# The mLSTM core of a hybrid layer: operands split into fp16 halves instead of fp32r halves, with one measured scale per head, and the query products ahead of the states

## The chip, the cores and the metric

The kernel runs on one core of one Trainium2 chip. The metric is the device time of one execution in microseconds (us); lower is better. Before the change three runs gave 1850.2, 1853.77 and 1854.75 us, the median is 1853.77. One further execution was profiled.

Engines: TensorE (PE; its weight loads are shown as PEld), VectorE (DVE), ScalarE (ACT), GpSimd (POOL) and SyncE (SP). SP issues most DMAs; a DMA that ScalarE issues stands in ScalarE's own instruction order (ACTq in the profile).

## The reference

One layer over 1024 latent tokens and 256 context tokens of width 1024, everything in fp32: a modulated norm, one input projection that feeds two branches (windowed attention and a bidirectional mLSTM), a gated merge, and a convolutional feed-forward block. What the change touches is the mLSTM, which runs in chunks of 128 tokens, in both directions, for 4 heads with 128 columns of query and key and 256 of value:

```python
def step(carry, xs):                       # one chunk of 128 tokens, one direction
    Cm, n, m = carry                       # state C (128 x 256), n (128), m
    ...
    s = jnp.einsum('bthd,bshd->bhts', qc, kc) * jnp.exp(dmat - m_t[..., None])
    num = (jnp.einsum('bhts,bshv->bthv', s, vc)
           + jnp.einsum('bthd,bhdv->bthv', qc, Cm) * w_inter.transpose(0, 2, 1)[..., None])
    nq = s.sum(axis=-1) + w_inter * jnp.einsum('bthd,bhd->bht', qc, n)
    den = jnp.maximum(jnp.abs(nq), jnp.exp(-m_t))
    h = num / den.transpose(0, 2, 1)[..., None]
    ...
    C_new = decay[..., None, None] * Cm + jnp.einsum('bshd,bshv->bhdv', kc * wk, vc)
    n_new = decay[..., None] * n + jnp.einsum('bshd->bhd', kc * wk)
```

The context chunks run first and give each direction its starting state; afterwards `h` of both directions is added, normalised per head (root mean square) and multiplied by a sigmoid gate.

## The kernel before, in words

The program has a start-up, an attention stage, the mLSTM stage (`stage_mlstm`, about 605 to 965 us of the trace) and a tail (`stage_tail`: the branch products yb and the feed-forward block).

Precision comes from halves: each operand x is split into hi = round(x) on ScalarE (`copy_act`, seen in the profile as L47) and lo = x - hi on VectorE (L54, or L56 where a scale is applied on the way). `mm3` (L158 to L165) then issues three matmuls for each product: hi.hi, hi.lo, lo.hi. Projection weights and the layer's input hT have fp16 halves that are scaled by a measured number. In the mLSTM core the halves of q, k, v, of the decayed scores and of the states are fp32r (32-bit) tiles.

Per head h, the stage does this, with the tile names that the profile shows:

- `prepare`, `load_kv`: load the weights (wrw_ml, wrw_mlqo), square them on ScalarE for their scale (wjw), split them (whkv, wlkv; whqo, wlqo).
- `proj_kv`: eight latent blocks, each 24 matmuls of 384 columns into a PSUM bank kv, of which there are two in turn. ScalarE takes out k and VH, VectorE VL. The two context blocks come by DMA as k and vr.
- `trans_k`: transposes of k into kT, split into kh, kl.
- `states`: the first two steps of each direction: kwh (GpSimd) and kwl (VectorE) are k times a decay, in halves; dC is their product with V; C is updated by VectorE and split into CH, CL.
- `proj_q`: q products in two banks of 512 columns, split into qh, ql.
- `core`: S = q.k in two banks; ub = S times decays (VectorE, L1460), split into sh, sl; then for each of eight blocks and both directions o (scores times V), i (q times state), nm (their sum and the division), hf (result), and the next dC, C, CH, CL.
- `proj_o`: the gate products mo, 96 matmuls of 512 columns, which the program writes behind the core and the scheduler places partly between the core's own products.
- `readout`, `turn`: squares of hf (rj), transposes mt, gate multiplication mo, stores to mlT_d on SP.
- `masked`, `decays`: the decay matrices ub of the next head, by DMA, an addition and 16 exponentials on ScalarE.
- `branch_sums`: sums of weights and activations for the tail (s_ba, t_at, s_bm); their loads are issued by ScalarE, into two buffers in turn, and their stores by SP.

The stage is written head by head in this order, and a scheduler that simulates the program orders every engine's instructions from it: each engine then executes its list strictly in order. The list depends on modelled durations, on priorities by program order and on when SBUF space is free, since pools of the next stage lie where earlier tiles lay. The tail's operand loads (baar, bawr on SP, L1717; sga on ScalarE's queue, L1748) wait for such space.

Of the kernel before, what the change touches and what calls it, by code (L numbers as in the profile page):

```python
# [348 lines left out]
def stage_startup(E, at):  # L349
# [3 lines left out]
    with ExitStack() as st:  # L353
# [198 lines left out]
        for i in range(4):  # L552
# [50 lines left out]
            for c in range(NCB):  # L603
                ps = pcx[c]
                kvx = wp.tile([P, 388], F32, tag="kvx", name=f"kvx{i}_{c}", bufs=3)
                a, z = i * 388, (i + 1) * 388
                mk, mv = min(max(512 - a, 0), 388), min(1536 - a, 388)
                if mk > 0:
                    copy_act(nc, kvx[:, :mk], ps[:, :mk], scale=DQK ** -0.5)
                    nc.sync.dma_start(E.kx_d[c][:, a : a + mk], kvx[:, :mk])  # L610
                if mk < mv:
                    nc.vector.tensor_copy(kvx[:, mk:mv], ps[:, mk:mv])
                    nc.sync.dma_start(E.vx_d[c][:, a + mk - 512 : a + mv - 512], kvx[:, mk:mv])
                if mv < 388:
                    nc.vector.tensor_tensor(E.gtile[:, c], ps[:, mv:388], E.gb, op=ALU.add)


def stage_attention(E, st, at):
# [343 lines left out]
    def gate_math():  # L962
# [102 lines left out]
        E.GC = dict(u_d=u_d, dec=dec, col=lambda nm, r: call[:, cols[nm] + r : cols[nm] + r + 1])  # L1065
# [36 lines left out]
    def early_act(j, ps):  # L1102
        E.kv0[j] = E.kvp.tile([P, 384], F32, name=f"kv0_{j}")
        copy_act(nc, E.kv0[j], ps[:, :384], scale=RAW["wf", NKV][:, 4:5])
# [146 lines left out]
def stage_mlstm(E, st):  # L1251
    nc, tc, A, ident, expo, hT, w2, dr = E.nc, E.tc, E.A, E.ident, E.expo, E.hT, E.w2, E.dr
    mm_tile, tp_tile, s_tile, mlT_d, gtile = E.mm_tile, E.tp_tile, E.s_tile, E.mlT_d, E.gtile

    E.turn_banks(3)
# [4 lines left out]
    vp = st.enter_context(tc.tile_pool(name="mlv", bufs=13, reuse_waits="tile"))  # L1260

# [6 lines left out]
    nc.gpsimd.memset(ones2[:, 0:1], 1.0)  # L1268

    def b512(name):  # L1270
        return bp.tile([P, 512], F32R, tag="b512", name=name)
# [8 lines left out]
    def v_tiles(h, j, src, scale=None):  # L1280
        vh = vp.tile([P, DVA], F32R, tag="VH", name=f"VH{h}_{j}")
        vl = vp.tile([P, DVA], F32R, tag="VL", name=f"VL{h}_{j}")
        nc.gpsimd.tensor_copy(vh[:, DV:DVA], ones2[:, 0:2])
        nc.gpsimd.tensor_copy(vl[:, DV:DVA], ones2[:, 2:4])
        split_from(nc, vh[:, 0:DV], vl[:, 0:DV], src, scale=scale)
        return vh, vl

    def prepare(h):
        H.setdefault(h, {})
        if h == 0:  # L1290
            H[h].update(w_ml=E.wml0, w_mlqo=E.wqo0)
# [16 lines left out]
    def proj_kv(h):  # L1308
        w, f = H[h].pop("wkv"), H[h]["fkv"]
        ks, vs = [None] * NBLK, [None] * NBLK  # L1310
        for j in orders(h)[0][1]:
            k = kp.tile([P, DQK], F32, tag="k", name=f"k{h}_{j}")
            if j < NCB:
                nc.sync.dma_start(k, E.kx_d[j][:, h * DQK : (h + 1) * DQK])
                vr = kp.tile([P, DV], F32, tag="vr", name=f"vr{h}_{j}", bufs=2)
                nc.sync.dma_start(vr, E.vx_d[j][:, h * DV : (h + 1) * DV])
                vs[j] = v_tiles(h, j, vr)
            elif h == 0 and j - NCB in E.kv0:
                kv = E.kv0[j - NCB]
                copy_act(nc, k, kv[:, 0:DQK], scale=DQK ** -0.5)  # L1320
                vs[j] = v_tiles(h, j, kv[:, 128:384])
            else:
                ps = mm_tile(f"kv{h}_{j}")
                mm3(nc, ps[:, :384], hT, w, sl((j - NCB) * P, P), sl(0, 384))
                kc = copy_act(nc, k, ps[:, 0:DQK], scale=f[:, 5:6])
                vs[j] = v_tiles(h, j, ps[:, 128:384], f[:, 4:5])
# [8 lines left out]
    def proj_q(h):  # L1335
# [4 lines left out]
        for t in range(2):  # L1340
# [3 lines left out]
            split_from(nc, qh, ql, ps, scale=f[:, 4:5])  # L1344
# [66 lines left out]
    def states(h):  # L1411
# [3 lines left out]
        CHL = [{}, {}]  # L1415

        def update(d, i, c):
# [3 lines left out]
            kh = wp.tile([P, DQK], F32R, tag="kwh", name=f"kwh{nm}", bufs=3)  # L1421
            kl = wp.tile([P, DQK], F32R, tag="kwl", name=f"kwl{nm}", bufs=3)
            wk = col("wK", r)
            E.kw = nc.gpsimd.tensor_scalar(kh, ks[c], wk, 1.0, op0=ALU.mult, op1=ALU.mult)  # L1424
            nc.vector.scalar_tensor_tensor(kl, ks[c], wk, kh.bitcast(F32), op0=ALU.mult, op1=ALU.subtract)
# [20 lines left out]
    def core(h):  # L1446
# [11 lines left out]
        for t, d in [(i ^ d, d) for i in range(2) for d, _ in orders(h)]:  # L1458
            Dm = DM.pop((h, t, d))
            nc.vector.tensor_tensor(Dm, pS[t].rearrange("p (c t) -> p c t", c=4)[:, :: (1, -1)[d]], Dm, op=ALU.mult)  # L1460
# [4 lines left out]
        def output(d, i, c, first):  # L1465
# [8 lines left out]
            num = wp.tile([P, 260], F32, tag="num", name=f"nm{nm}", bufs=3)  # L1474
            nc.scalar.activation(num[:, :257], pi[:, :257], AF.Copy, scale=col("wI", r))
            nc.vector.tensor_tensor(num[:, :257], num[:, :257], ps[:, :257], op=ALU.add)
            nq = num[:, 256:257]
            nc.vector.scalar_tensor_tensor(num[:, 257:258], nq, -1.0, col("em", r), op0=ALU.mult, op1=ALU.max)
# [20 lines left out]
    def readout(h):  # L1499
        hf, sgs = H[h]["hf"], H[h]["sg"]  # L1500
        for t in halves(h):
# [6 lines left out]
            nc.gpsimd.tensor_scalar(rr[:, 0:4], rr[:, 0:4], 1.0 / DV, EPS, op0=ALU.mult, op1=ALU.add)  # L1508
# [61 lines left out]
    for h in range(MLH):  # L1570
# [866 lines left out]
```

## Time and profile before

| | |
|---|---|
| runs | 1853.77 us median (1850.2 to 1854.75) |
| profiled execution | 1858.65 us, of which the span of the trace is 1856.9 |
| busy share of the span | PE 97%, DVE 76%, ACT 58%, POOL 27% |
| TensorE's granted clock, mean | 0.987 |
| mLSTM stage | about 605 to 965 us |
| heads' cores, first S to last o or i | about 631 to 671, 733 to 765, 825 to 863 and 920 to 953 us |

Two things matter in reading it. TensorE's matmuls overlap, so a busy TensorE is not one at its peak: the interval from one start to the next is the price of a matmul, not its duration. And the granted clock falls to one half for some us after TensorE has stood still, so a stall costs more than its own length. In a row of the groups stand the busy time and the mean duration in ns, then the idle time of that engine ahead of it, and what ended it.

### The profile page before, as it was taken

What the parts mean: (1) busy time and instruction counts of PE and PEld (TensorE: products, weight loads), DVE (VectorE), ACT (ScalarE), POOL (GpSimd) and SP (SyncE); (2) the same over time, 40 slices, a digit from 0 to 9 for tenths busy, and PEclk for the clock granted to TensorE, in tenths of its full rate; (3) what the DMA queues carried; (4) which work ended last, traced back from release to release, by engine and by line L of the source; (5) the groups of instructions that cost most, each with busy time, mean ns of one, the idle gap of its engine ahead of it and who ended that gap; (6) DMA issues with size and microseconds to landing.
All of it is one profiled execution on the core that took longest, in us unless ns stands there. A gap on an engine that the chain in (4) does not pass through costs nothing.

```text
span 1856.9 us, 27874 instructions
## 1 busy us (share of the span) xinstructions
PE 1795.2 (97%) x9207; PEld 1286.0 (69%) x9207; DVE 1418.6 (76%) x2864; ACT 1070.7 (58%) x2229; POOL 510.5 (27%) x747
## 2 busy tenths in 40 slices
PE   7889999999998899989999999999999999999999
PEld 3855555555555565656668887878888888888887
DVE  3848878888788685858687787698988998896665
ACT  4747777878787564646356563375444444464441
POOL 2467769687762630303020021000000000000000
PEclk9899999999999899999999999999999999999999
DMA  8647988888787724260449936413454544599751
GB/s 336 234 138 147 195 174 177 190 179 196 148 181 138 217 94 161 79 210 32 148 160 359 362 101 221 168 57 125 159 211 180 186 172 154 197 321 369 262 171 68
DMA packets 302193, 342.47 MB, mean 184 GB/s; under 512 B 176208, under 2 KB 200672, under 8 KB 299232
## 3 DMA queue, kind: packets, MB, share of 16 engines
q1 hardware_dynamic: 287648, 314.47, 56.1%
q10 hardware_dynamic: 14400, 26.22, 4.3%
q8 instruction: 72, 1.18, 0.3%
q14 instruction: 73, 0.60, 0.1%
HBM read 224.61 MB, written 76.16 MB: 162 GB/s over the span
## 4 chain that ended last, share of the span: by engine, by line
PE 77%; DVE 7%; DMA 5%; ACT 5%; issue 4%; POOL 3%; ACTq 0%; SPq 0%; POOLq 0%; DVEq 0%
PE g L706 8%; PE pq L706 6%; PE pa L2015 4%; PE pa L2017 4%; PE pa L2016 4%; PE po L706 3%; PE dx L2015 2%; PE dx L2017 2%; PE dx L2016 2%; PE pb L2017 2%; PE pb L2016 2%; PE pb L2015 2%; PE yb L2015 2%; PE yb L2016 2%; PE yb L2017 2%
## 5 line engine op out<-in xcount | busy, mean ns | idle before, releaser
L850 DVE CUSTOM_DVE_ANT_0 s<-s,maskA,nsink 128x640 f32<-128x640 f32 (+1 forms) x128 | 117.5, 918 | 75.0 <-PE s L845 74.6
L866 DVE TENSOR_TENSOR P<-s,P 128x640 f16<-128x640 f32 (+1 forms) x128 | 100.7, 787 | 1.0 <-ACT s L861 1.0
L860 ACT ACTIVATE P<-s,st 128x640 f16<-128x640 f32 (+1 forms) x128 | 98.3, 768 | 4.2
L706 PE MATMUL g<-hH,fh 128*128 128x512 f16 x256 | 97.9, 382 | 0.0
L706 PE MATMUL g<-hH,fl 128*128 128x512 f16 x256 | 97.8, 382 | 0.0
L706 PE MATMUL g<-hL,fh 128*128 128x512 f16 x256 | 97.7, 382 | 0.0
L861 ACT ACTIVATE s<-s,st 128x640 f32<-128x640 f32 (+1 forms) x128 | 93.9, 734 | 0.0
L706 PEld LDWEIGHTS <-hH 128*128 128x128 f16 x640 | 62.1, 98 | 36.5 <-DVE t L770 0.4
L858 ACT ACTIVATE st<-st,shift 128x1 f32<-128x1 f32 x128 | 37.6, 294 | 85.4 <-DVE st L850 84.7
L706 PE MATMUL pq<-wha,hH 128*128 128x384 f16 (+1 forms) x256 | 83.9, 328 | 0.1
L706 PE MATMUL pq<-wha,hL 128*128 128x384 f16 (+1 forms) x256 | 83.9, 328 | 0.0
L706 PE MATMUL pq<-wla,hH 128*128 128x384 f16 (+1 forms) x256 | 83.9, 328 | 0.0
L706 PEld LDWEIGHTS <-fh 128*128 128x128 f16 x512 | 48.1, 99 | 47.9 <-issue 1.6
L2153 ACT ACTIVATE cv<-ua,vecT 128x1024 f32<-128x1024 f32 x22 | 27.4, 1246 | 83.9 <-DVE ua L2126 83.9
L1424 POOL TENSOR_SCALAR kwh<-k,gcall 128x128 fp32r<-128x128 f32 x72 | 33.1, 463 | 154.4 <-PE dC L164 57.1
L163 PE MATMUL kv<-whkv,hH 128*128 128x384 f16 x192 | 63.3, 330 | 6.0 <-DVE VL L56 6.0
L2015 PE MATMUL dx<-dwh,dfh 128*128 128x512 f32 (+1 forms) x176 | 68.3, 388 | 0.0
L2017 PE MATMUL dx<-dwh,dfl 128*128 128x512 f32 (+1 forms) x176 | 68.2, 388 | 0.0
L2016 PE MATMUL dx<-dwl,dfh 128*128 128x512 f32 (+1 forms) x176 | 68.2, 387 | 0.0
L47 ACT ACTIVATE dfh<-drf 128x512 fp32r<-128x512 f32 x55 | 34.3, 628 | 58.5 <-PE dx L2016 26.0
L54 DVE TENSOR_TENSOR dfl<-drf,dfh 128x512 fp32r<-128x512 f32 x55 | 37.7, 691 | 36.5 <-ACT dfh L47 36.4
L164 PE MATMUL kv<-wlkv,hH 128*128 128x384 f16 x192 | 63.2, 329 | 0.4
(691 smaller groups left out, 6253.8 us busy)
## 6 DMA issues: line engine op xcount, KB each, us to landing
ur<-in_w_up SPq DMA_DIRECT2D x22, 1024.0 KB
wmb<-in_w_modB SPq DMA_DIRECT2D x48, 256.0 KB
f_d<-cv SPq DMA_DIRECT2D x22, 512.0 KB
wm<-in_w_modA SPq DMA_DIRECT2D x16, 512.0 KB
fr<-in_w_g SPq DMA_DIRECT2D x32, 256.0 KB
drf<-fs_d SPq DMA_DIRECT2D x15, 512.0 KB
drw<-wt_d SPq DMA_DIRECT2D x14, 512.0 KB
w1b<-in_w_cx SPq DMA_DIRECT2D x16, 388.0 KB
```

The lines of the kernel that those rows point to most:

```text
L54: rest = nc.vector.tensor_tensor(lo, src, whole, op=ALU.subtract)
L163: nc.tensor.matmul(ps, lh[:, ls], rh[:, rs], start=start and i == 0, stop=False)
L164: nc.tensor.matmul(ps, lh[:, ls], rl[:, rs], start=False, stop=False)
L706: nc.tensor.matmul(self.ps, x, w, start=self.i == 0, stop=self.i == self.n - 1)
L850: nc.vector.tensor_tensor_reduce(e, e, self.mask, scale=self.ss[:, h : h + 1], scalar=nsink[:, hh : hh + 1], op0=ALU.add, op1=ALU.min, acc ...
L858: nc.scalar.activation(m, st4[:, 8 + h : 9 + h], AF.Identity, bias=shift)
L860: nc.scalar.activation(two[:, :W], e, AF.Exp, bias=m, scale=-1.0)
L861: nc.scalar.activation(e, e, AF.Exp, bias=m, scale=-1.0, accum_out=st4[:, 4 + h : 5 + h])
L866: nc.vector.tensor_tensor(two[:, W : 2 * W], self.e[h], two[:, :W], op=ALU.subtract)
L2015: nc.tensor.matmul(ps, lh, rh, start=start and i == 0, stop=False, skip_group_check=True)
L2016: nc.tensor.matmul(ps, lh, rl, start=False, stop=False, skip_group_check=True)
L2017: nc.tensor.matmul(ps, ll, rh, start=False, stop=stop and i == n - 1, skip_group_check=True)
```

## The change

- The halves of k, v, q, kT, of ub (sh, sl), of kw and of the states are fp16 tiles instead of fp32r. A weight load of TensorE is then a load of 16-bit weights.
- k, v and q leave PSUM times 2^-15 instead of times the weights' own factor, so that they fit fp16; the constants that need that factor (the floor of the denominator, the EPS of the norm) are multiplied accordingly in a few one-column operations on GpSimd. The column of ones in V is 16.
- One scale per head is measured: ScalarE squares every k|v block (kvj, 384 columns) and both halves of q (qj, 512 columns) with an accumulated sum, a small matmul (mlq) adds over the partitions, and three one-column VectorE operations end in hc[:,7:8], the reciprocal. The states are split with that factor (CL becomes a scalar_tensor_tensor), and the scores are multiplied by it and the decay in one scalar_tensor_tensor (ub).
- The context blocks come as one tile of k and v and pass through the same k copy, split and square as the latent ones.
- `proj_q` of the next head is written ahead of `states` of the next head.

```diff
     def b512(name):
-        return bp.tile([P, 512], F32R, tag="b512", name=name)
+        return bp.tile([P, 512], F16, tag="b512", name=name)
...
     def proj_kv(h):
+        def square(j, src, scale):
+            junk = rp.tile([P, 384], BF16, tag="kvj", name=f"kvj{h}_{j}", bufs=1)
+            nc.scalar.activation(junk, src, AF.Square, scale=scale, accum_out=q[:, j : j + 1])
...
-                kc = copy_act(nc, k, ps[:, 0:DQK], scale=f[:, 5:6])
-                vs[j] = v_tiles(h, j, ps[:, 128:384], f[:, 4:5])
+                src, scale = mm_tile(f"kv{h}_{j}"), 2.0 ** -15
+                mm3(nc, src[:, :384], hT, w, sl((j - NCB) * P, P), sl(0, 384))
+            kc = copy_act(nc, k, src[:, 0:DQK], scale=scale)
+            vs[j] = v_tiles(h, j, src[:, 128:384], None if scale == 1.0 else scale)
+            square(j, src[:, :384], scale)
...
     def proj_q(h):
-            split_from(nc, qh, ql, ps, scale=f[:, 4:5])
+            split_from(nc, qh, ql, ps, scale=2.0 ** -15)
+            junk = rp.tile([P, 512], BF16, tag="qj", name=f"qj{h}_{t}", bufs=1)
+            nc.scalar.activation(junk, ps, AF.Square, scale=2.0 ** -15, accum_out=H[h]["sq"][:, NBLK + t : NBLK + t + 1])
...
     def states(h):
+        hc = H[h]["c"]
+        pb = tp_tile(f"mlq{h}")
+        nc.tensor.matmul(pb[:, : NBLK + 2], E.ones, H[h]["sq"], start=True, stop=True)
+        nc.vector.tensor_reduce(hc[:, 5:6], pb[:, : NBLK + 2], axis=AX.X, op=ALU.add)
+        nc.vector.tensor_scalar(hc[:, 6:7], hc[:, 5:6], NT * ONE ** 2, 2.0 ** -16, op0=ALU.add, op1=ALU.mult)
+        nc.vector.reciprocal(hc[:, 7:8], hc[:, 6:7])
...
-                ch = wp.tile([P, DVA], F32R, tag=f"CH{d}", name=f"CH{nm}", bufs=3)
-                cl = wp.tile([P, DVA], F32R, tag=f"CL{d}", name=f"CL{nm}", bufs=3)
-                split_from(nc, ch, cl, Cs[d])
+                ch = wp.tile([P, DVA], F16, tag=f"CH{d}", name=f"CH{nm}", bufs=3)
+                cl = wp.tile([P, DVA], F16, tag=f"CL{d}", name=f"CL{nm}", bufs=3)
+                split_from(nc, ch, cl, Cs[d], scale=hc[:, 7:8])
...
     def core(h):
-            nc.vector.tensor_tensor(Dm, pS[t].rearrange("p (c t) -> p c t", c=4)[:, :: (1, -1)[d]], Dm, op=ALU.mult)
+            nc.vector.scalar_tensor_tensor(
+                Dm, pS[t].rearrange("p (c t) -> p c t", c=4)[:, :: (1, -1)[d]], hd["c"][:, 7:8], Dm, op0=ALU.mult, op1=ALU.mult
+            )
...
             proj_kv(h + 1)
             trans_k(h + 1)
+            proj_q(h + 1)
             states(h + 1)
...
-            proj_q(h + 1)
```

The engines' lists change in more places than the diff shows. On VectorE at the start of head 1's core, before (the digit behind a name is the head; ql is the low half of q, ub the decayed scores):

```order
L56 SCALAR_TENSOR_TENSOR ql1_1_9020<-q1_1_8994,wfw_mlqo1_8517,qh1_1_9019 128x512
L1460 TENSOR_TENSOR ub1_0_0_8544<-S1_0_9065,ub1_0_0_8544 128x512
L1460 TENSOR_TENSOR ub1_0_1_8547<-S1_0_9065,ub1_0_1_8547 128x512
L1460 TENSOR_TENSOR ub1_1_1_8541<-S1_1_9078,ub1_1_1_8541 128x512
L1460 TENSOR_TENSOR ub1_1_0_8550<-S1_1_9078,ub1_1_0_8550 128x512
```

and now:

```order
L56 SCALAR_TENSOR_TENSOR ql1_1_9046<-q1_1_9020,qh1_1_9045 128x512
L1450 SCALAR_TENSOR_TENSOR kwl1_1_3_9250<-k1_8_8694,gcall_1202,kwh1_1_3_9249 128x128
L1450 SCALAR_TENSOR_TENSOR kwl1_0_3_9263<-k1_3_8885,gcall_1202,kwh1_0_3_9262 128x128
L1450 SCALAR_TENSOR_TENSOR kwl1_1_4_9306<-k1_7_8729,gcall_1202,kwh1_1_4_9305 128x128
L1436 TENSOR_REDUCE mlc1_8566<-mlq1_9051 128x1
L1437 TENSOR_SCALAR mlc1_8566<-mlc1_8566 128x1
L1438 RECIPROCAL mlc1_8566<-mlc1_8566 128x1
L1485 SCALAR_TENSOR_TENSOR ub1_0_0_8592<-S1_0_9146,mlc1_8566,ub1_0_0_8592 128x512
L56 SCALAR_TENSOR_TENSOR CL1_1_1_9088<-C1_1_0_9066,mlc1_8566,CH1_1_1_9087 128x258
L56 SCALAR_TENSOR_TENSOR CL1_0_1_9101<-C1_0_0_9076,mlc1_8566,CH1_0_1_9100 128x258
L1485 SCALAR_TENSOR_TENSOR ub1_1_1_8589<-S1_1_9159,mlc1_8566,ub1_1_1_8589 128x512
```

The scale (mlc) stands between ql and the first ub, and two CL, which stood ahead of the q halves before, stand between the ubs.

On ScalarE at the start of head 2's core, before (s_bm are the loads that ScalarE issues):

```order
L47 ACTIVATE qh2_0_10188<-q2_0_10163,wfw_mlqo2_9715 128x512
L1538 DMA s_bm0_0_10263<-in_w_bm 128x512 x2
L1538 DMA s_bm0_1_10264<-in_w_bm 128x512
L47 ACTIVATE qh2_1_10217<-q2_1_10192,wfw_mlqo2_9715 128x512
L1538 DMA s_bm0_1_10264<-in_w_bm 128x512
L47 ACTIVATE sh2_0_0_10304<-ub2_0_0_9739 128x512
```

and now:

```order
L47 ACTIVATE qh2_0_10251<-q2_0_10226 128x512
L1361 ACTIVATE qj2_0_10255,mlq2_9809<-q2_0_10226 128x512
L1566 DMA s_bm0_0_10383<-in_w_bm 128x512 x2
L47 ACTIVATE qh2_1_10282<-q2_1_10257 128x512
L1566 DMA s_bm0_1_10384<-in_w_bm 128x512 x2
L1361 ACTIVATE qj2_1_10286,mlq2_9809<-q2_1_10257 128x512
L47 ACTIVATE CH2_0_1_10324<-C2_0_0_10303,mlc2_9803 128x258
```

All four s_bm issues stand ahead of the last square, qj, and a split of the states follows it.

On SP at the end of head 3, before (baar, bawr: the operands of the tail's first products; mlT_d: head 3's results):

```order
L1717 DMA bawr1_12179<-in_w_ba 128x1024
L1717 DMA baar0_12189<-attT_d_64 128x2x512
L1717 DMA baar1_12199<-attT_d_64 128x2x512
L1717 DMA baar2_12225<-attT_d_64 128x2x512
L1717 DMA bawr2_12235<-in_w_ba 128x1024
L1717 DMA baar3_12277<-attT_d_64 128x2x512
L1717 DMA bawr3_12287<-in_w_ba 128x1024
L1523 DMA mlT_d_65<-mo3_0_0_12085 128x512
```

and now:

```order
L1745 DMA bawr1_12339<-in_w_ba 128x1024
L1551 DMA mlT_d_65<-mo3_0_0_12244 128x512
L1551 DMA mlT_d_65<-mo3_0_1_12252 128x512
L1551 DMA mlT_d_65<-mo3_1_0_12260 128x512
L1551 DMA mlT_d_65<-mo3_1_1_12268 128x512
L1745 DMA baar0_12349<-attT_d_64 128x2x512
L1745 DMA baar1_12359<-attT_d_64 128x2x512
```

The first baar load stands behind the four stores; before, four of them stood ahead. The tail's first sga loads moved the other way, into head 0's core on ScalarE's queue.

More of the change, by code (lines that the diff above doesn't have):

```diff
@@ L608, in stage_startup @@
                 if mk > 0:
-                    copy_act(nc, kvx[:, :mk], ps[:, :mk], scale=DQK ** -0.5)
+                    copy_act(nc, kvx[:, :mk], ps[:, :mk])
                     nc.sync.dma_start(E.kx_d[c][:, a : a + mk], kvx[:, :mk])
@@ L1103, in early_act @@
         E.kv0[j] = E.kvp.tile([P, 384], F32, name=f"kv0_{j}")
-        copy_act(nc, E.kv0[j], ps[:, :384], scale=RAW["wf", NKV][:, 4:5])
+        copy_act(nc, E.kv0[j], ps[:, :384], scale=2.0 ** -15)
     def gate_slots(c):
@@ L1253, in stage_mlstm @@
     mm_tile, tp_tile, s_tile, mlT_d, gtile = E.mm_tile, E.tp_tile, E.s_tile, E.mlT_d, E.gtile
+    ONE = 16.0
     E.turn_banks(3)
```

53 lines of the change are left out of this document (31 added, 22 removed).

## The prediction

> **What bounds the kernel now.** I read the totals, then the windows by stage, then what TensorE waits for from the mLSTM stage to the tail, then single places in the timeline.
>
> ```profile
> PE 1795.2 (97%) x9207; PEld 1286.0 (69%) x9207; DVE 1418.6 (76%) x2864; ACT 1070.7 (58%) x2229; POOL 510.5 (27%) x747
> 680.00:720.00 40.00, 35.95 (x216) 21.90 (x215) 23.47 (x43) 26.24 (x57) 3.18 (x9) 0.96 0.59 200
> 740.00:760.00 20.00, 19.93 (x129) 15.63 (x128) 18.83 (x76) 9.88 (x23) 10.16 (x26) 1.00 0.17 49
> 975.00:1855.00 880.00, 876.56 (x3901) 722.87 (x3899) 704.62 (x997) 429.97 (x679) 24.80 (x20) 1.00 0.56 203
> ```
>
> Columns of the windows: length, busy PE, PEld, DVE, ACT, POOL with counts, granted clock, DMA share, GB/s. TensorE is busy 97%, but the changed stage (605 to 965) is not one thing. In a head's core (740 to 760 in head 1) VectorE has 18.83 of 20 us: it is nearly as full as TensorE there. Between heads (680 to 720) ScalarE has 26.24 of 40. From 975 on TensorE is busy 876.56 of 880, so whatever is lost before stays lost.
>
> ```profile
> PE kv L163 <- DVE VL L56: 6.0, 4, 2.6
> PE q L163 <- DVE o L1233: 3.2, 1, 3.2
> PE yb L2015 <- ACT bawh L47: 2.5, 1, 2.5
> PE S L163 <- DVE ql L56: 2.2, 3, 1.6
> PE o L163 <- ACT sh L47: 1.5, 1, 1.5
> ```
>
> TensorE's stalls (us, times, longest) lie at the heads' borders and at the tail's first product.
>
> **The change part by part.** *TensorE on fp16.* Operands of S, o, i and dC are 16-bit now.
>
> ```profile
> 736.75 0.28 PE L163 MATMUL i<-CH,qh 128*128 128x258 f32 x1
> 736.87 0.29 PE L164 MATMUL i<-CL,qh 128*128 128x258 f32 x1
> ...
> 400.32 0.27 PE L844 MATMUL s<-KcA,QT 128*128 128x256 f16 x1
> 400.43 0.27 PE L845 MATMUL s<-KcB,QT 128*128 128x256 f16 x1
> ...
> 734.74 0.28 PE L164 MATMUL S<-ql,kh 128*128 128x128 f32 x1
> 734.85 0.27 PE L165 MATMUL S<-qh,kl 128*128 128x128 f32 x1
> ...
> L165 PEld LDWEIGHTS <-hL 128*128 128x128 f16 x192 | 18.9, 99 | 13.3 <-issue 1.3
> L164 PEld LDWEIGHTS dC<-VL,kwh 128*128 128x128 f32 x72 | 14.1, 196 | 0.4
> ...
> 959.97 0.38 PE L164 MATMUL mo<-hL,whqo 128*128 128x512 f16 x1
> 960.19 0.38 PE L165 MATMUL mo<-hH,wlqo 128*128 128x512 f16 x1
> ```
>
> A 258-column fp32r product starts every 0.12 us, a 256-column fp16 one every 0.11: 600 of them (192 o, 192 i, 216 dC) save 600 x 0.01 = 6 us of TensorE. S starts every 0.11; an fp16 weight load takes 0.099 against 0.196, so S goes to between 0.055 (half of the 256-column interval) and 0.099: 96 x 0.011 to 0.055 = 1 to 5 us. If TensorE alone set the time, 7 to 11 us would be won. The Trainium skill (TensorE: Matmul & The Clock Gate, Back-to-back issue gap) has 81 ns for a 128-column product in a stream with weight loads; by that S would save 96 x 0.03 = 3 us, inside these bounds.
>
> But VectorE fills the core. What TensorE gains there it waits again for C, CL and nm; only the pure row of mo products behind each core can shrink, because more mo fit between. The order has 43, 44, 42 and 42 of them after the last o or i, against 44, 48, 46 and 48: 15 fewer x 0.215 = **-3.2 us** (bounds: 0 if the core stretches, -11 if TensorE is the limit).
>
> *VectorE in the core.* Scaling by the measured number turns two-operand forms into three-operand ones.
>
> ```profile
> L1460 DVE TENSOR_TENSOR ub<-S,ub 128x512 f32<-128x512 f32 x16 | 10.3, 682 | 0.9 <-PE S L165 0.9
> L56 DVE SCALAR_TENSOR_TENSOR ql<-q,wfw_mlqo,qh 128x512 fp32r<-128x512 f32 x6 | 4.5, 749 | 11.0 <-ACT qh L47 11.0
> L54 DVE TENSOR_TENSOR CL<-C,CH 128x258 fp32r<-128x258 f32 x64 | 27.2, 439 | 2.3 <-ACT CH L47 1.9
> L1432 DVE SCALAR_TENSOR_TENSOR C<-C,dec,dC 128x258 f32<-128x258 f32 x64 | 29.7, 475 | 7.2 <-PE dC L165 6.9
> L1478 DVE SCALAR_TENSOR_TENSOR nm<-nm,gcall 128x1 f32<-128x1 f32 x64 | 9.5, 152 | 0.1
> ```
>
> Per head: 4 ub at 0.749 for 0.682 (+0.27), 16 CL at 0.475 for 0.439 (+0.58), 3 one-column operations that make the scale (about 0.1 each in a row, +0.3): 1.1 us, for four heads 4.4. Then the start. Nothing may be scaled before the second q half is squared:
>
> ```profile
> 732.63 0.38 PE L165 MATMUL q<-hH,wlqo 128*128 128x512 f16 x1
> ...
> 733.05 0.69 ACT L47 ACTIVATE qh<-q,wfw_mlqo 128x512 fp32r<-128x512 f32 x1 [4.43 <-PE q L165]
> ...
> 734.44 1.28 DVE L1460 TENSOR_TENSOR ub<-S,ub 128x512 f32<-128x512 f32 x2
> ...
> 737.64 0.39 PE L163 MATMUL o<-VH,sh 128*128 128x258 f32 x1
> ```
>
> Now the first ub starts 1.4 us after q ends (733.0), the first o at 4.6. After: qh to 0.7, qj (0.7 like qh, and a read of 0.19) to 1.5, mlq to 1.8, three small operations to 2.3, then ub, two CL that formerly stood ahead of ub, the next ub, sh 0.6: o at about 5.3. With what else is pushed behind I take 0.9 for each of heads 1 to 3: 2.7. Together **+7.1** (0, if VectorE's small gaps swallow it, to +10). The S saving is hidden by this same wait, so it is not counted again.
>
> *ScalarE between heads.* New: ten squares of 384 columns, two of 512, two k copies.
>
> ```profile
> L1507 ACT ACTIVATE rj<-hf 128x256 f32<-128x256 f32 x32 | 12.9, 404 | 3.4 <-DVE hf L1484 3.2
> L1507 ACT ACTIVATION_READ_ACCUMULATOR rj<-hf 128x1 f32 x32 | 6.0, 188 | 0.0
> L112 ACT ACTIVATE wjw_mlqo<-wrw_mlqo 128x768 bf16<-128x768 f32 x12 | 10.1, 840 | 5.2 <-DMA wrw_mlqo<-in_w_mlqo 5.0
> L47 ACT ACTIVATE k<-kv,wfw_ml 128x128 f32<-128x128 f32 x24 | 8.6, 360 | 34.4 <-PE kv L165 34.4
> ```
>
> A square of 384 lies a quarter of the way from 0.404 to 0.840: 0.51, and about 0.1 of its read is not covered: 0.6. Per head 10 x 0.6 + 2 x 0.8 + 2 x 0.36 = 8.3 us, 33 in all, in 40 us windows with 14 us idle. Most is hidden under kv products. But the square is one more reader of the kv bank, of which there are two, and the wait of kv for VL (6.0 us now) then waits for it as well. Two squares at 0.6 stand in the queue at each such place; I take **+2** in all (0 to +6).
>
> *The queue at head 2.*
>
> ```profile
> 822.01 4.53 ACTq L1538 DMA_DIRECT2D s_bm<-in_w_bm  x3
> 826.59 0.69 ACT L47 ACTIVATE qh<-q,wfw_mlqo 128x512 fp32r<-128x512 f32 x1 [5.80 <-DMA s_bm<-in_w_bm]
> ```
>
> ScalarE issues the s_bm loads itself, and they wait for buffers; qh sits behind three of them for 5.80 us. In the new order all four issues stand ahead of qj, and the scale, all ub and all CL hang on qj, where today two ub run before: **+1.5** (0 to +4).
>
> *Head 0.* The first s_ba round moves ahead of the stage, so ScalarE's early block goes, but a run of squares follows in its place: **-1** (-3 to +2), guessed from the 3.2 us stall of the first q product, which I don't price closer.
>
> *The tail's loads.* Smaller tiles move the pools, and with them what a load waits for.
>
> ```profile
> 945.93 7.06 SPq L1717 DMA_DIRECT2D baar<-attT_d  x3
> ...
> 963.00 2.10 PE L1520 MATMUL mt<-ident,hf 128*128 128x128 f32 x16
> 967.57 0.80 PE L2015 MATMUL yb<-baah,bawh 128*128 128x512 f32 x1 [2.48 <-ACT bawh L47]
> ...
> 973.78 0.47 PE L2016 MATMUL yb<-baal,bawh 128*128 128x512 f32 x1
> ...
>   DMA baar<-t_at_d: 2.1, 1
> ```
>
> Today three baar loads go out in a row from 945.93 on, under head 3's core, and yb starts 2.48 us after the last mt (965.1). In the new order every baar load stands behind the four mlT_d stores, which wait for mt: four mo, three-operand forms of 512 columns like ql, at 0.75 end about 1.5 us after mt, since the first overlap it; the stores go out until about 2.3 (an estimate); the load takes some 2.1 (the last row: what ScalarE waits for a baar load today); baah and baal follow at 0.6 and 0.7: yb at about 6, **+3.5** (0 to +6). After today's stall TensorE runs at half clock until 973.78, 6.2 us, which costs 3.1; the longer stall pays that once, as now. The Trainium skill (the same page, What's actually happening) gives about 3.4 us of work to come back to full clock; the row has nearly twice that, so the row is used.
>
> Sum: -3.2 + 7.1 + 2 + 1.5 - 1 + 3.5 = **+9.9 us**. The profiled execution (span 1856.9, with 1.75 outside 1858.65) goes to 1868.5. It lies 4.9 above the median of the runs, 1853.77; for the median I add the same: **1864**.
>
> **The rivals.** (1) *TensorE is the limit in the core*: the 2 of 20 us that VectorE has free there are enough. For it: TensorE shows 19.93 of 20. Against it: VectorE's work rises. Then -7 to -11 for fp16, no core loss, and the border terms +6 shrink to +2: about -7, **1847**. (2) *The additions are hidden*: VectorE's gaps take the 1.1 us a head, the squares lie in ScalarE's idle 14 of 40 us, baar comes in time: -3.2 + 2.7 + 1.5 = +1, **1855**. (3) *The clock falls at each core's start.*
>
> ```profile
> 834.00:837.00 3.00, 3.00 (x12) 1.99 (x11) 2.70 (x6) 2.53 (x6) 0.00 (x0) 0.50 0.46 158
> ```
>
> Behind the stalls of 1.6 (S for ql) and 1.5 us (o for sh) that end at 832 the clock was 0.50 here. If the wait for the scale does that at heads 1 and 3 too, each pays up to 3 us more: +6, **1870**. The Trainium skill (the same page, What's actually happening) has the gate close after an idle window of about 3.4 us; the row's gate closed on stalls that are each under half of it.
>
> **How the numbers follow.** Within 0.3%, about what a measurement of this kernel tells from no change, is 1848.2 to 1859.3. The forecast has 0.39 (0.05 of it still the same, 0.34 slower), rival 1 0.27 (its 1847 lies at the lower bound: 0.19 faster, 0.08 the same), rival 2 0.22 (0.02 faster, 0.15 the same, 0.05 slower), rival 3 0.12, all slower. That gives faster 0.21, same 0.28, slower 0.51. The range: rival 1 with the whole 11 and border terms of 2 is 1845; the forecast with the upper ends of VectorE's, the border's, head 2's and the tail's terms (2.9 + 4 + 2.5 + 2.5 = 12) is 1876. I take 1844 to 1877. The likeliest case alone spans 1858 to 1872.
>
> **What would show it.** Right: the windows of the cores stay as long or grow although S, o, i and dC start 0.11 apart or less; VectorE stays above 18 of 20; the first o waits for sh at each head; yb starts 5 us or more after mt. Wrong: cores shorter by 2 us each (rival 1), a yb stall of 2.5 us as now, no wait of kv for a square. The forecast falls if the stage from 605 to 965 is shorter in the new trace.

## The result, and the profile after

The changed kernel takes 1868.29 us (median of five runs, 1866.46 to 1870.54) against 1853.77 us: a ratio of 1.0076, 95% interval 1.0053 to 1.0098, so it is slower by 0.5 to 1.0%. Its profiled execution took 1868.29 us, with a span of 1866.2. The traces differ by 9.3 us, the medians by 14.5, because the profiled execution of the kernel before lay 4.9 above its median; what those 4.9 us are cannot be seen in one trace, and the places below add up to the 9.3.

The totals of the page after, and then the waits of TensorE from 600 to 990 us (total us, times, longest):

```profile
PE 1783.6 (96%) x9215; PEld 1258.1 (67%) x9215; DVE 1428.2 (77%) x2876; ACT 1098.6 (59%) x2333; POOL 533.9 (29%) x767
```

```profile
PE yb L2043 <- ACT baah L47: 10.0, 1, 10.0
PE kv L163 <- ACT kvj L1325: 4.7, 5, 1.6
PE i L163 <- ACT CH L47: 4.4, 5, 2.6
PE kv L164 <- DVE wlkv L56: 4.4, 3, 1.5
PE kT L1370 <- ACT k L47: 4.0, 3, 2.8
PE o L163 <- ACT sh L47: 4.0, 3, 1.3
```

TensorE is busy 11.6 us less and the kernel takes longer: the work went, and waits took its place. The tail's first product waits 10.0 us where it waited 2.5; kv waits for the new squares; i and o wait for splits that hang on the scale.

Where the time went, from the starts in the two timelines (the first transpose mt ends a head):

| stretch | before | after | difference |
|---|---|---|---|
| to the first mt of head 0 | 680.5 | 678.1 | -2.4 |
| head 1 (mt to mt) | 95.3 | 94.3 | -1.0 |
| head 2 | 97.3 | 99.2 | +1.8 |
| head 3 | 89.9 | 95.1 | +5.2 |
| mt of head 3 to the first yb | 4.6 | 12.1 | +7.6 |
| the tail from there | 889.3 | 887.4 | -1.9 |

The products became as short as was read ahead. The timeline of S and dC after, in head 1, then the windows of the cores of heads 1, 2 and 3 after, then those of heads 1 and 3 before (length, busy PE, PEld, DVE, ACT, POOL, granted clock, DMA share, GB/s):

```profile
728.88 0.22 PE L164 MATMUL S<-ql,kh 128*128 128x128 f16 x1
728.94 0.22 PE L165 MATMUL S<-qh,kl 128*128 128x128 f16 x1
...
729.61 0.27 PE L164 MATMUL dC<-VL,kwh 128*128 128x258 f16 x1
729.72 0.27 PE L165 MATMUL dC<-VH,kwl 128*128 128x258 f16 x1
```

```profile
729.00:763.00 34.00, 30.27 (x219) 19.62 (x217) 32.87 (x117) 19.67 (x41) 15.08 (x39) 1.00 0.14 32
823.40:862.00 38.60, 33.10 (x224) 20.82 (x223) 35.09 (x120) 19.38 (x45) 13.67 (x36) 0.91 0.25 79
921.00:958.00 37.00, 33.53 (x228) 21.14 (x227) 33.96 (x120) 19.88 (x41) 9.57 (x22) 0.95 0.05 15
```

```profile
733.00:765.00 32.00, 31.65 (x211) 25.09 (x209) 29.56 (x108) 16.61 (x38) 13.70 (x36) 1.00 0.12 34
920.50:953.00 32.50, 32.16 (x212) 25.46 (x211) 30.02 (x110) 17.57 (x38) 8.65 (x19) 1.00 0.15 50
```

S starts every 0.056 us instead of 0.11, dC every 0.11 instead of 0.12. VectorE went from 29.56 of 32 to 32.87 of 34 us in head 1. In head 3 the clock fell to 0.95 as well, where it had been 1.00.

### The profile page after: what moved, and what is told of

Read it like the earlier page. It is cut to its first block, busy times and chain, and to the rows that moved or that the text cites. A ratio compares the mean times of both kernels' runs of the same rounds, so it can differ in the third digit from the quotient of the medians.

```text
span 1866.2 us, 27945 instructions
## 1 busy us (share of the span) xinstructions
PE 1783.6 (96%) x9215; PEld 1258.1 (67%) x9215; DVE 1428.2 (77%) x2876; ACT 1098.6 (59%) x2333; POOL 533.9 (29%) x767
## 4 chain that ended last, share of the span: by engine, by line
PE 77%; DVE 8%; ACT 4%; DMA 4%; POOL 4%; issue 3%; SPq 0%; POOLq 0%; ACTq 0%; DVEq 0%
PE g L706 8%; PE pq L706 6%; PE pa L2043 4%; PE pa L2044 4%; PE pa L2045 4%; PE po L706 3%; PE yb L2043 2%; PE yb L2044 2%; PE yb L2045 2%; PE dx L2043 2%; PE dx L2045 2%; PE dx L2044 2%; PE pb L2044 2%; PE pb L2045 2%; PE pb L2043 2%
## 5 line engine op out<-in xcount | busy, mean ns | idle before, releaser
L706 PE MATMUL g<-hH,fh 128*128 128x512 f16 x256 | 98.2, 384 | 0.0
L1449 POOL TENSOR_SCALAR kwh<-k,gcall 128x128 f16<-128x128 f32 x72 | 44.6, 623 | 175.7 <-PE dC L164 82.0
```

Of the source, the lines that this page charges most:

```text
L706: nc.tensor.matmul(self.ps, x, w, start=self.i == 0, stop=self.i == self.n - 1)
```

## The experiments

Each run is compared with runs of the kernel before on the same chip. The runs take the change apart from its end: first the late loads, then the squares, the scaled forms, the place of q, and last the data type.

| run | median us | before us | ratio (95%) |
|---|---|---|---|
| the change | 1868.29 | 1853.77 | 1.0076 (1.0053 to 1.0098) |
| t1, early baar loads | 1861.42 | 1852.51 | 1.0051 (1.0036 to 1.0066) |
| t2, and squares ahead of the splits | 1852.91 | 1853.22 | 0.9999 (0.9986 to 1.0012) |
| t3, t1 without squares | 1855.15 | 1852.51 | 1.0012 (1.0001 to 1.0022) |
| t4, and two-operand forms | 1850.06 | 1852.51 | 0.9990 (0.9980 to 1.0000) |
| t5, and q behind the states | 1845.46 | 1852.51 | 0.9958 (0.9942 to 0.9975) |
| t6, t5 with fixed scales | 1845.69 | 1853.22 | 0.9962 (0.9947 to 0.9977) |
| t6q, t6 with q ahead | 1851.46 | 1853.22 | 0.9990 (0.9977 to 1.0002) |
| t7, t6 with VectorE's ub mask | 1845.60 | 1853.22 | 0.9961 (0.9950 to 0.9973) |
| t8, t6 with fp32r halves | 1858.60 | 1853.64 | 1.0036 (1.0023 to 1.0049) |
| t9, t6 with kwh on ScalarE | 1838.12 | 1853.64 | 0.9914 (0.9898 to 0.9929) |
| t10, t2 with kwh on ScalarE | 1851.10 | 1853.14 | 0.9993 (0.9980 to 1.0006) |
| b9, before with kwh on ScalarE | 1849.39 | 1853.14 | 0.9980 (0.9970 to 0.9990) |

### t1: the tail's loads early again

```diff
+    st.enter_context(tc.tile_pool(name="mlpad", bufs=1, reuse_waits="tile")).tile([P, 6144], F32, name="mlpad")
     rp = st.enter_context(tc.tile_pool(name="mlr", bufs=2, reuse_waits="tile"))
```

The unused 24 KB move the pool of hf, sg and mo to where the tail's baar tiles do not lie.

> The changed kernel with an unused 24 KB pool ahead of the pool of hf, sg and mo, so that the tail's first four baar loads stand ahead of the last mlT_d stores again. Theory: the first yb product waits about 2.5 us as before instead of 10.0, and the time falls by 6 to 8 us, to about 1861. Rival (the loads are bound by bandwidth, the delay only moves to a later yb): the stall of the first yb shrinks but the time falls by less than 2 us, above 1866.

The ratio fell by 0.0025, 4.6 us of 1853 (6.9 by the medians). The intervals of the two ratios overlap, so the times alone leave the size open; what became of the stall is seen in the traces. SP, ScalarE, VectorE and TensorE in the changed kernel:

```profile
968.09 4.00 SPq L1551 DMA_DIRECT2D mlT_d<-mo  x4
972.21 1.44 SPq L1745 DMA_DIRECT2D baar<-attT_d  x3
...
978.14 3.73 ACT L47 ACTIVATE baah<-baar 128x512 fp32r<-128x512 f32 x6 [2.52 <-DMA baar<-attT_d]
...
970.26 1.41 DVE L1550 SCALAR_TENSOR_TENSOR mo<-mt,mlw,sg 128x512 f32<-128x512 f32 x2 [0.34 <-DMA mlT_d<-mo]
...
966.67 2.10 PE L1548 MATMUL mt<-ident,hf 128*128 128x128 f32 x16
978.82 0.79 PE L2043 MATMUL yb<-baah,bawh 128*128 128x512 f32 x1 [10.05 <-ACT baah L47]
```

and SP and TensorE in t1:

```profile
959.48 1.60 SPq L1746 DMA_DIRECT2D baar<-attT_d  x3
...
968.45 2.10 PE L1548 MATMUL mt<-ident,hf 128*128 128x128 f32 x16
973.03 0.50 PE L2044 MATMUL yb<-baah,bawh 128*128 128x512 f32 x1 [2.48 <-ACT bawh L47]
```

The chain of the 10 us stands in the rows: mt ends at 968.8; the third mo waits for the first store (mo has two buffers); the last store goes out at 972.1, the first baar load at 972.2; the first baah starts at 978.1. With the loads early the wait is 2.48 us, as in the kernel before. From the first mt of head 3 to the end t1 takes 893.7 us and the changed kernel 899.5, so most of the 7.6 us stays won: the theory, and not a delay that only moves on.

### t2: the squares ahead of the splits

```diff
             kc = copy_act(nc, k, src[:, 0:DQK], scale=scale)
+            square(j, src[:, :384], scale)
             vs[j] = v_tiles(h, j, src[:, 128:384], None if scale == 1.0 else scale)
-            square(j, src[:, :384], scale)
...
+            junk = rp.tile([P, 512], BF16, tag="qj", name=f"qj{h}_{t}", bufs=1)
+            nc.scalar.activation(junk, ps, AF.Square, scale=2.0 ** -15, accum_out=H[h]["sq"][:, NBLK + t : NBLK + t + 1])
             split_from(nc, qh, ql, ps, scale=2.0 ** -15)
-            junk = rp.tile([P, 512], BF16, tag="qj", name=f"qj{h}_{t}", bufs=1)
-            nc.scalar.activation(junk, ps, AF.Square, scale=2.0 ** -15, accum_out=H[h]["sq"][:, NBLK + t : NBLK + t + 1])
```

> The changed kernel with early baar loads (the first run, 1861.4), and each square stands ahead of the split of the same bank, so that ScalarE no longer waits for VL and ql before it. Theory (half of what the squares cost is that wait, 12.8 us of it ahead of kvj and 8.6 ahead of qj): 2 to 4 us faster than the first run, about 1858.5. Rival (the squares cost their own ScalarE time, wherever they stand): within 1 us of it.

It was more than the theory asked for: 1861.42 to 1852.91, ratio 1.0051 to 0.9999. The groups of ScalarE in the changed kernel, then in t2 (count, busy us, mean ns, idle time ahead and who ended it):

```profile
L1325 ACT ACTIVATE kvj<-kv 128x384 bf16<-128x384 f32 x32 | 15.9, 495 | 12.9 <-DVE VL L56 12.8
L1361 ACT ACTIVATE qj<-q 128x512 bf16<-128x512 f32 x8 | 4.8, 595 | 8.6 <-DVE ql L56 8.6
```

```profile
L1325 ACT ACTIVATE kvj<-kv 128x384 bf16<-128x384 f32 x32 | 15.6, 488 | 0.0
L1360 ACT ACTIVATE qj<-q 128x512 bf16<-128x512 f32 x8 | 4.7, 592 | 23.3 <-PE q L165 23.3
```

The squares take the same time in both. What cost was that a square, which only reads its bank, was made to wait until VectorE's VL or ql had read the same bank; ScalarE stood in its strict order behind it for 21 us, and k, VH and qh of the next bank stood behind that. Standing first, the square waits for nothing but its product.

### t3: no squares, the scale a constant

```diff
-            square(j, src[:, :384], scale)
...
-            nc.scalar.activation(junk, ps, AF.Square, scale=2.0 ** -15, accum_out=H[h]["sq"][:, NBLK + t : NBLK + t + 1])
...
-        nc.tensor.matmul(pb[:, : NBLK + 2], E.ones, H[h]["sq"], start=True, stop=True)
-        nc.vector.tensor_reduce(hc[:, 5:6], pb[:, : NBLK + 2], axis=AX.X, op=ALU.add)
-        nc.vector.tensor_scalar(hc[:, 6:7], hc[:, 5:6], NT * ONE ** 2, 2.0 ** -16, op0=ALU.add, op1=ALU.mult)
-        nc.vector.reciprocal(hc[:, 7:8], hc[:, 6:7])
...
+        nc.gpsimd.memset(c[:, 7:8], 2.0 ** -11)
```

> As the run before, but without kvj, qj, the mlq matmul and the three VectorE operations behind it: the scale is a constant, all other forms stay. Theory: the squares on ScalarE and the wait for the scale at each core's start cost 5 to 8 us, so 1853 to 1856, and the waits of kv for kvj and of i for CH at the start of a core go. Rival (the three-operand forms of ub and CL cost the most): at most 2 us less than with the squares, 1859 or more.

The ratio fell from 1.0051 to 1.0012 (7.2 us), as the theory said. But t2, which keeps all squares, is no slower than t3: the intervals of 0.9999 and 1.0012 overlap. So the time of the squares, and the operations behind them, cost nothing that these runs can tell; their place cost 7 to 10 us by the ratios (t1 to t3, t1 to t2).

### t4: no scaling of ub and the states

```diff
-            nc.vector.scalar_tensor_tensor(
-                Dm, pS[t].rearrange("p (c t) -> p c t", c=4)[:, :: (1, -1)[d]], hd["c"][:, 7:8], Dm, op0=ALU.mult, op1=ALU.mult
-            )
+            nc.vector.tensor_tensor(Dm, pS[t].rearrange("p (c t) -> p c t", c=4)[:, :: (1, -1)[d]], Dm, op=ALU.mult)
...
-                split_from(nc, ch, cl, Cs[d], scale=hc[:, 7:8])
+                split_from(nc, ch, cl, Cs[d])
```

In t4 and t5 the scores and the states are not scaled while the floor of the denominator still is: this part of the computation is changed, so that their output is not the reference's. Nothing of the work is left out but the scaling itself.

> As the run before, and ub and the states are not scaled at all: tensor_tensor forms as in the kernel before, no per-partition scale in CH and CL. Theory: 64 CL, 64 CH and 16 ub get cheaper by 0.07 to 0.09 us, VectorE loses about 1.1 us per head, the time falls by 3 to 5 us to 1849 to 1852. Rival (VectorE is not the limit in the core): no change, within 1 us.

The ratio fell by 0.0022, 4.1 us: the theory. The groups of t3, then of t4:

```profile
L56 DVE SCALAR_TENSOR_TENSOR CL<-C,mlc,CH 128x258 f16<-128x258 f32 x64 | 31.1, 496 | 4.0 <-ACT CH L47 3.6
L47 ACT ACTIVATE CH<-C,mlc 128x258 f16<-128x258 f32 x64 | 31.5, 504 | 18.5 <-DVE C L1448 16.9 <-DVE nm L1499 1.3 <-DVE nm L1497 0.2
```

```profile
L54 DVE TENSOR_TENSOR CL<-C,CH 128x258 f16<-128x258 f32 x64 | 26.6, 424 | 2.2 <-ACT CH L47 1.5
L47 ACT ACTIVATE CH<-C 128x258 f16<-128x258 f32 x64 | 25.9, 416 | 24.4 <-DVE C L1448 23.8 <-DVE nm L1495 0.2
```

Both halves of a state pay: 0.07 us on VectorE and 0.09 on ScalarE, one behind the other on the way from C to the next i.

### t5: q behind the states again

```diff
             trans_k(h + 1)
-            proj_q(h + 1)
             states(h + 1)
...
+            proj_q(h + 1)
             for _ in range((3, 4, 3)[h]):
```

> As the run before, and the query products stand behind the states again, as in the kernel before: the fp16 halves almost alone. Theory: the core is filled by VectorE, so fp16 saves 2 to 4 us against the kernel before, 1850 to 1852; the place of q changes less than 2 us. Rival (TensorE is the limit in the core): 1843 to 1847.

1845.46 us, ratio 0.9958: neither the 1850 to 1852 of the theory nor a place of q that is worth less than 2 us. The rival's numbers were right. Two things were open: whether q's place costs 5 us, since the profiled spans of t4 and t5 (1848.8 and 1849.8) did not show it, and whether fp16 is what saves.

### t6 and t6q: fixed scales, with q behind and ahead

```diff
+    SK, SQ = 2.0 ** -5, 2.0 ** -6
...
-        nc.gpsimd.memset(c[:, 7:8], 2.0 ** -11)
+        nc.gpsimd.tensor_scalar(c[:, 5:6], c[:, 0:1], SK, None, op0=ALU.mult)
...
-            kc = copy_act(nc, k, src[:, 0:DQK], scale=scale)
+            kc = copy_act(nc, k, src[:, 0:DQK], scale=c[:, 5:6] if j < NCB else scale * SK)
...
-            split_from(nc, qh, ql, ps, scale=2.0 ** -15)
+            split_from(nc, qh, ql, ps, scale=2.0 ** -15 * SQ)
...
-        nc.gpsimd.tensor_scalar(em, GC["both"]("em", h), hc[:, 4:5], hc[:, 7:8], op0=ALU.mult, op1=ALU.mult)
+        nc.gpsimd.tensor_scalar(em, GC["both"]("em", h), hc[:, 4:5], None, op0=ALU.mult)
```

> The fp16 halves with early baar loads and q behind the states, no squares and no measured scale: k is stored times 2^-5 and q times 2^-6 more instead, and the floor of the denominator takes both factors. It computes all that the reference computes. Theory: as fast as the run with fp16 alone, 1844 to 1849, and so faster than both kernels. Rival (that run's median of four was a lucky one; its profiled span was 1849.8): 1850 to 1853, no different from the kernel before.

> The run before with the query products ahead of the states, as in the change. Theory from the traces of the two runs without squares, in which every head took the same time but for head 0: within 2 us of the run before. Rival (the medians, 1850.1 against 1845.5): 4 to 5 us slower.

t6 takes 1845.69 us, ratio 0.9962: faster than both kernels. It gives up what the change measures: its two factors are chosen for these inputs, and no run here shows how far others may lie from them. With q ahead it takes 1851.46, ratio 0.9990, so q's place costs 0.0028 or 5.2 us, and the theory that was read from the two single traces fell. In the traces of this pair heads 1 to 3 take 92.0, 99.8 and 89.6 us with q ahead and 90.1, 98.2 and 87.9 with q behind, 1.6 to 1.9 us each. In the core the order shows: with q behind, the first two states are finished under the q products; with q ahead, VectorE has their C and CL to do when it should make ub. TensorE's wait for sh ahead of the first o is 1.0 us in heads 1 and 3 with q ahead and below 0.3 with q behind. From the end of q to the last mo it is 43.0 us against 39.8 in head 1, but a part of that only moved: with q ahead, products of the first states stand in this stretch too.

### t8: the same program with fp32r halves

```diff
-        return bp.tile([P, 512], F16, tag="b512", name=name)
+        return bp.tile([P, 512], F32R, tag="b512", name=name)
```

The tiles VH, VL, kwh, kwl, CH and CL change in the same way.

> The run with fixed scales, but with fp32r halves again (and without the unused pool, for which there is no room then): constant scales, the context blocks through ScalarE, q behind the states. It tells the data type from the cheaper constant scales. Theory (the 7 us came from TensorE, so TensorE was the limit in the core after all): no faster than the kernel before, 1852 to 1855. Rival (half of it came from VL, k, VH and ql, which are 0.06 to 0.09 us shorter with a constant scale): 1848 to 1850.

1858.60 us: fp32r halves in this program are slower by 12.9 us (ratio 1.0036 against 0.9962, 0.0074), so without fp16 nothing of the saving is left. The 12.9 us are not the price of the type in the kernel before. The theory had a bound of 1855; that this program lies 6.7 us (0.0036) above the kernel before in fp32r was expected by neither, and I did not find out what in it costs that. What the constant scales bring by themselves is not told apart either. Of the 12.2 us between the spans of t8 and t6, 5.2 lie ahead of the first mt of head 0, where S waits 3.8 us for kl in t8. VectorE's C, and the window of head 1's core, in t8:

```profile
L1449 DVE SCALAR_TENSOR_TENSOR C<-C,dec,dC 128x258 f32<-128x258 f32 x64 | 29.8, 476 | 3.7 <-PE dC L165 3.6
```

```profile
734.00:766.00 32.00, 31.76 (x211) 25.16 (x211) 29.97 (x110) 16.17 (x37) 12.66 (x35) 1.00 0.14 34
```

and in t6:

```profile
L1449 DVE SCALAR_TENSOR_TENSOR C<-C,dec,dC 128x258 f32<-128x258 f32 x64 | 29.7, 473 | 0.5 <-PE dC L165 0.3
```

```profile
727.50:760.00 32.50, 31.51 (x223) 19.91 (x221) 30.51 (x115) 18.86 (x39) 12.21 (x35) 1.00 0.11 34
```

The row of the kernel before stands in the prediction: 7.2 us idle ahead of C, 6.9 of it for PE's dC. In t8 it is 3.6, in t6 0.3. That is summed over all heads, and only 3.5 of the 7.2 us lie in windows around the four cores, 0.6 in head 1's, so this row does not price the saving. VectorE's share is 94% in both windows, and head 1's core takes 32 us with either type. What differs is what else the core holds. From the timelines, the core (first S to last o or i), the mo products behind it, and both together (first S to first mt). Heads 0 and 2 hold stalls with the half clock, so heads 1 and 3 are shown:

| | head 1: core, mo behind it, together | head 3: core, mo behind it, together |
|---|---|---|
| before | 32.2 us, 48, 43.1 us | 32.4 us, 48, 42.9 us |
| t8 | 32.0 us, 48, 42.8 us | 32.2 us, 48, 42.7 us |
| t6 | 32.1 us, 35, 40.2 us | 30.0 us, 44, 39.6 us |
| the change | 33.6 us, 44, 43.5 us | 36.1 us, 42, 45.3 us |

The windows from first S to first mt of head 1, before and then in t6:

```profile
732.66:775.75 43.09, 42.74 (x265) 30.58 (x263) 36.21 (x134) 23.68 (x59) 16.64 (x42) 1.00 0.09 27
```

```profile
727.08:767.23 40.15, 39.16 (x264) 23.86 (x262) 34.57 (x129) 23.12 (x57) 14.98 (x39) 1.00 0.09 27
```

Before, TensorE is busy 42.74 of 43.09 us in this stretch, VectorE 36.21. With fp16 TensorE has some 3 us less to do in it (an estimate: 24 S at 0.056 less, 138 o, i and dC at 0.010 to 0.012 less), and the stretch is 2.9 us shorter. In head 1 this shows as 13 more mo products in a core of the same length, in head 3 as a core that is 2.2 us shorter than t8's and 4 more mo products in it. So over the core and the mo products together it was TensorE that set the time, although VectorE is nearly full in the core.

### t9, t10 and b9: kwh on ScalarE

```diff
-            E.kw = nc.gpsimd.tensor_scalar(kh, ks[c], wk, 1.0, op0=ALU.mult, op1=ALU.mult)
+            E.kw = copy_act(nc, kh, ks[c], scale=wk)
```

> The run with fixed scales, and kwh, the high half of the decayed key, is made by ScalarE instead of GpSimd (72 of 0.46 us there). Theory (kwl on VectorE waits for GpSimd, and ScalarE has half its time free in the core): 1 to 3 us faster, 1843 to 1845. Rival (ScalarE's queue puts nm and CH later, on which o, i and the states wait): 1 to 4 us slower.

> The changed kernel with its measured scale, early baar loads, squares ahead of the splits, and kwh made by ScalarE. Theory (kwh on ScalarE brings less GpSimd work at every head): 4 to 8 us faster than without it (1852.9), 1845 to 1849. Rival (its 7 us in the kernel with fixed scales came from one place, a stall of 2.7 us and the half clock behind it at head 2, which this kernel does not have): within 2 us of 1852.9.

> The kernel before, with kwh made by ScalarE and nothing else. Theory: the gain does not depend on the halves' type, 1846 to 1850. Rival (it came from one place in the other kernel's order): 1852 to 1856.

t9 takes 1838.12 us, 0.86% under the kernel before and the best of all; the theory had 1 to 3 us and got 7.6. A stall in t6 explains most of it: its timeline at head 2, and the window behind it:

```profile
812.56 0.28 PE L165 MATMUL dC<-VH,kwl 128*128 128x258 f16 x1 [2.69 <-DVE kwl L1442]
```

```profile
813.00:817.00 4.00, 4.00 (x13) 1.45 (x11) 3.77 (x10) 0.42 (x1) 0.73 (x2) 0.57 0.53 199
```

dC waits 2.69 us for kwl, and TensorE then runs at half clock. In t9's order there is no such stall at head 2, which takes 93.1 us there against 98.2; heads 1 and 3 take the same time in both to 0.5 us, and head 0 is 2.5 shorter. t9 has such a wait too (4.6 us), at the start of head 0's core. So it is not GpSimd's work at every head. t10 gains 1.8 us by the medians with overlapping intervals: its rival. b9 gains 0.0020 or 3.7 us and lies in its theory's range, so about half of the gain comes in the fp32r kernel too. Where b9 wins cannot be told well, as the one trace of the kernel before lay 4.9 us above its median.

### t7: head 0's mask on VectorE

```diff
-                eng, late = (nc.vector, E.wkv) if h else (nc.gpsimd, E.kw)
+                eng, late = (nc.vector, E.wkv) if h else (nc.vector, E.kw)
```

> The run with fixed scales, and head 0's four additions of the mask to ub are done by VectorE instead of GpSimd. In the trace of fp16 alone VectorE's VL took 1.4 us instead of 0.42 while GpSimd did these additions, and dC waited 9.0 us for C. Theory (the two engines hinder each other): VL back to 0.42, the wait of dC below 6 us, 2 to 4 us faster than with fixed scales. Rival (dC waits for C because of VectorE's order, not of its speed): no gain, within 1 us.

No gain (1845.60 against 1845.69): the rival. The slowing itself is real. In t5 VectorE's VL took 1.44 us each while GpSimd added the mask, and in t7, without it, 0.41:

```profile
629.75 2.88 DVE L54 TENSOR_TENSOR VL<-kv,VH 128x256 f16<-128x256 f32 x2
...
626.59 5.76 POOL L1410 TENSOR_TENSOR ub<-ub,mlmask 128x512 f32<-128x512 f32 x4
```

```profile
L54 DVE TENSOR_TENSOR VL<-kv,VH 128x256 f16<-128x256 f32 x8 | 3.1, 410 | 0.0
```

But t7 starts from t6, and there nothing was left to win: in t6 GpSimd's additions start at 630.2 us, behind head 0's last VL, whose mean is 0.43 already, and dC waits 2.4 us for C instead of the 9.0 of t5. In t7 S waits 3.8 us for kh in its place, and the first mt of head 0 comes at 676.9 us against 677.1. So what the slowing costs in the order of t5 is not shown.

## Why the prediction was right or wrong, point by point

The forecast was 1864 us, between 1844 and 1877, and most likely slower; it is 1868.3 and slower. The sign and the range held, and the signs that were named came: the cores of heads 1 to 3 are longer (33.6 against 32.2 us in head 1), the first o waits 1.3 us for sh in each of them, kv waits for squares and yb for baah. That the sum of +9.9 came so near to +14.5 is in part luck: two errors of opposite sign stood in it.

**TensorE on fp16: the step that failed.** The intervals came out as read: 0.11 for o, i and dC, and 0.056 for S, at the low end of the stated 0.055 to 0.099. The Trainium skill's 81 ns for a 128-column product in such a stream (TensorE: Matmul & The Clock Gate, Back-to-back issue gap) was too long here. But "What TensorE gains there it waits again for C, CL and nm", and with it -3.2 us, was wrong. fp16 alone saved 0.0042 to 0.0038 (t5, t6), some 7 us, the low end of the first rival's -7 to -11. The row of mo products did shrink as said, from 186 to 168 in t5 and t6, which is 3.9 us at 0.215; but head 3's core shrank too, from 32.4 to 30.0 us, and from first S to first mt heads 1 and 3 won 2.9 and 3.3 us, about what TensorE saved there. A share of 18.83 in 20 us was read as the limit; TensorE's 19.93 in the same row was the one that set the time. In the change itself this gain is lost again to the waits for the scale: the same stretch takes 43.5 and 45.3 us.

**VectorE in the core: right, with the sizes nearly.** Of the 4.4 us for the forms, ub and CL were 3.4, and together with CH they cost 4.1 (t3 to t4); the rest, the operations that make the scale, went with the squares in t3. ub took 0.745 us as forecast; CL 0.505 instead of 0.475, and CH on ScalarE went from 0.415 to 0.504, which the prediction had left out. The start of the core was put at 0.9 us for each of three heads. The scale in head 1, after (q ends at 728.7):

```profile
728.28 0.38 PE L165 MATMUL q<-hH,wlqo 128*128 128x512 f16 x1
...
730.15 0.60 ACT L1361 ACTIVATE qj<-q 128x512 bf16<-128x512 f32 x1 [0.85 <-DVE ql L56]
...
731.91 0.75 DVE L1485 SCALAR_TENSOR_TENSOR ub<-S,mlc,ub 128x512 f32<-128x512 f32 x1
...
734.83 0.28 PE L163 MATMUL o<-VH,sh 128*128 128x258 f16 x1 [1.34 <-ACT sh L47]
```

The first ub started 3.2 us after q, not 2.3, and o 6.2, not 5.3, because qj waited 0.85 us for ql, the other reader of its bank. The displaced work was undersized: q's place alone costs 5.2 to 5.9 us (t6q to t6, t4 to t5) where the whole start was put at 2.7.

**ScalarE between heads: the mechanism was half right, the size wrong.** That a square is one more reader of the bank, and that kv then waits for it, is what the trace shows (4.7 us). But +2 was worked out from the squares' own time. They cost 7 to 10 us (t1 to t3, t1 to t2) by a wait that was not foreseen, and none by their time.

**The queue at head 2** was put at +1.5, and it did not come about. ScalarE in the changed kernel:

```profile
823.40 0.60 ACT L47 ACTIVATE qh<-q 128x512 f16<-128x512 f32 x1 [2.91 <-PE q L165]
823.54 0.82 ACTq L1566 DMA_DIRECT2D s_bm<-in_w_bm  x2
824.85 0.60 ACT L1361 ACTIVATE qj<-q 128x512 bf16<-128x512 f32 x1 [0.85 <-DVE ql L56]
```

The s_bm loads no longer wait: qh starts as q ends, and qj waits for ql alone, 0.85 us as in head 1. What made head 2 1.8 us longer is therefore not this queue; the stretch from mt of head 1 to the end of head 2's q, where kv waits for squares, is 1.6 us longer (51.0 against 49.4), but no run took that apart.

**Head 0** was guessed at -1 and came to -2.4, its core included.

**The tail's loads: the mechanism was right, the size half.** +3.5 was put for it, and the wait grew by 7.6 us; t1 gives 4.6 (ratios) to 6.9 (medians). The chain was right. Two of its links were undersized: the stores went out until 3.3 us after mt and not 2.3, since the third mo waited for a buffer, and the load, from its issue to the first baah, took 5.9 us and not 2.1. The 2.1 was ScalarE's idle time ahead of another load, not the time of a load; and here three loads of 512 KB went out within 1.44 us, while the DMA engines were 96 to 98% busy. The half clock was paid once, as said, and for less: TensorE's clock was back at 1.00 some 3.4 us after the first yb, where the kernel before needed 6.2.

**The rivals.** The first (TensorE is the limit) was right on fp16 and wrong that the rest is small. The second, that the additions are hidden, holds for the squares' time, once they stand first. The third, the clock at the cores' starts, happened in part: the clock was 0.91 and 0.95 in the cores of heads 2 and 3, which had 0.96 and 1.00 before, and 1.00 in head 1's as before.

Put together from the ratios, in us of 1853: fp16 alone -7.4, q ahead +5.6, scaled forms +4.1, squares behind the splits +7.2, late loads +4.6; the sum is 14.1, against 14.5. It closes by construction, since each step starts where the last one ended, so it is no check; and the steps' sizes hold for this order of taking them out.

## What to carry to other kernels

An engine that is 94% busy is not yet the one that limits: where two are nearly full, look over a stretch that takes in the work that can move, here the core with the mo products behind it, and see which of them never stands still. A new reader of a buffer cost here by where it stands in the order, not by its duration: put it ahead of the reader on the other engine. And after a change of tile sizes, compare where the next stage's loads stand in the DMA queue, since that alone moved about 5 us here, and an unused pool gave it back.

## What the runs showed of the hardware

- A scale that is read per partition costs more than a constant one: k 0.360 against 0.277 us, VH 0.464 against 0.384, ql 0.749 against 0.685, VL 0.482 against 0.420 (kernel before, and after), and CH 0.504 against 0.416 (t3, t4). The data type is not the reason: t8, with constants and fp32r halves, has 0.276, 0.382, 0.688 and 0.419 for the first four.
- VectorE's subtraction with both inputs in SBUF slowed from 0.41 to 1.44 us while GpSimd added two SBUF tiles. The Trainium skill (GPSIMD Engine Reference, the row on SBUF interfaces) says that the two engines share these interfaces, with contention where VectorE has two SBUF inputs; the trace agrees.
- fp16 128-column products with a weight load each start every 0.056 us, half of the fp32r ones.
- kwh on GpSimd took 0.62 us on average in the changed kernel and 0.46 in t3 to t6, with the same shape and type. The medians are 0.39 and 0.37: in the changed kernel three of the 72 took 3.86 us each, and in each of these VectorE did the four additions of the mask to ub, which also have both inputs in SBUF, one after the other.
- Not every stall lowers TensorE's clock. In the kernel before it was 0.50 behind a wait of 2.64 us (711.3 to 714.5 us) and 1.00 behind one of 2.48 (805.2 to 809).
